# Two experts share one strip of 64 token slots in a mixture-of-experts encoder block

## The chip, the cores and the metric

The kernel runs on one core of a Trainium2 chip. The metric is the device time of one execution in microseconds (us). TensorE multiplies matrices, VectorE (DVE), ScalarE (ACT) and GpSimd (POOL) work elementwise, and SyncE (SP) issues all DMAs of this kernel.

## The reference

One layer of an encoder with 512 tokens of 1024 channels, all in float32. A first half mixes the tokens (a convolution module and a state-space scan, merged by gates). The second half, the one that the change is about, sends every token to two of 64 experts: the best of 8 groups, and in it the best two of 8 experts.

```
def _hier_moe(xt, w_grp, b_grp, w_er, b_er, w1, w3, w2):
    gp = softmax(xt @ w_grp + b_grp);  g_p, g_idx = top_k(gp, 1)
    el = (xt @ w_er + b_er).reshape(t, 8, 8);  el_sel = el of the group chosen
    e_p, e_loc = top_k(softmax(el_sel), 2);  e_p = e_p / sum(e_p)
    weights = g_p * e_p;  e_glob = g_idx * 8 + e_loc
    ...
    def expert_block(args):
        xblk, e = args
        hdn = jax.nn.silu(xblk @ w1[e]) * (xblk @ w3[e])
        return hdn @ w2[e]
    ...
# reference: h = h + g2 * moe;  return rmsnorm(h, final_g)
```

w1[e] and w3[e] are 1024 x 512, w2[e] is 512 x 1024: 6.29 MB an expert, 403 MB for all. With 512 x 2 assignments an expert has 16 tokens on average.

## The kernel before

The first half (some 765 us) computes everything up to h, the residual stream, and hg, the normalized tokens, both with tokens on the partitions. Then the router chooses groups and experts for all tokens on DVE. `pcum` counts, with products of one-hots and a triangular matrix in PSUM, which place a token has in the queue of its expert; the key of an assignment is 512 times its expert plus that place. Every expert has a strip of 64 slots (CAP). Assignments beyond them are counted in `nq`, and a loop behind the main one works them off, with passes of 128 slots that load their expert's weights again; with no such assignment it is skipped.

**The expert loop** (lines 1471 to 1505) goes over 32 pairs of experts. A pair has 128 slots, 64 for each. For each pair:
- `choose` (DVE) makes the one-hot S [tokens, slots] from the keys; `gather` multiplies it with hg on TensorE, 8 steps (k) of 4 products into ps_g, and ACT writes the gathered tokens xg, scaled and shifted, in FP32. From pair 3 on the one-hot is bf16 and hg is split into three bf16 parts by `split`, so that a step has 12 bf16 products in place of 4 FP32 ones.
- `hidden` multiplies 64 columns of xg with w1 and w3 of one expert, 16 products into ps_w; ACT makes the SiLU (`sl`), DVE multiplies. `hidden_t` transposes the result into ps_ht, DVE copies it to `ht`. `second` multiplies ht with w2, 8 products into the two halves ps_y. The second expert of a pair has them crossed, so that each of the two PSUM tiles holds 64 rows of either expert.
- `scale_y` multiplies by the routing weights (tables tabA, tabB by slot) and g2, splits y into two parts yh and yl, and POOL makes `so`, the one-hot back from slots to tokens. `combine` has 8 steps: two products into ps_o and an addition to h on DVE. For the last pair, two of the four token blocks are summed in PSUM instead (ps_f), where `to_psum` puts h.

The generators gather (g, G for the first), combine (c; the `tables` in pair 0), split (x) and to_psum (z) are advanced one step at a time between the matmuls of `hidden`, and while ACT, DVE work on its result. FILL0 to FILL3 and FILL are the lists of these steps: for each expert of the pair, ten places: before each k of `hidden`, after it (place 8) and after `hidden_t` (place 9).

**The weights** come through a ring of 8 buffers of 2 MB (`load_upto`, lines 750 to 775). An expert has 3 blocks: the first and the second half of k of w1 and w3 together, and w2. A load waits until the products that read its buffer last are done. Blocks 8 to 23 and the last expert's are loaded in smaller pieces (`fine`). All loads are issued by SP in order. Six of the first eight blocks are loaded during the first half.

The end (`final`) is the last RMSNorm, per block of 128 tokens, and the store.

Of the kernel before, what the change touches and what calls it, by code (L numbers as in the profile page):

```python
# [129 lines left out]
def hybrid_block(ctx: ExitStack, tc: tile.TileContext, a, out, dbg=None, stage=9):  # L130
# [1130 lines left out]

    def split():
        h1 = tk.tile([P, 4, KD, P], BF, name="hg1", tag="hg1")
        hgb = hg.bitcast(BF).rearrange("p c k (r q) -> p c k r q", r=2)
# [2 lines left out]
        todo = [(c, slice(4 * q, 4 * q + 4)) for q in range(2) for c in range(4)]
        ts = {}
        for n in range(len(todo) + 1):
            if n < len(todo):  # L1270
                i = todo[n]
                S.copy(h1[:, i[0], i[1]], hg[:, i[0], i[1]])
                ts[n] = mo.tile([P, 4, P], F32, name="hs", tag="S", bufs=2)
                V.tensor_sub(ts[n], hg[:, i[0], i[1]], h1[:, i[0], i[1]])
# [430 lines left out]
```

## Time and profile before

| | us |
|---|---|
| median of 3 runs (1839.68 to 1841.95) | 1841.07 |
| the profiled execution | 1842.43 |
| its span, from the first to the last instruction | 1840.6 |
| TensorE busy in it | 1752.0 |
| DVE busy in it | 1067.2 |

The profile is one execution. Its rows give start and duration of instructions, merged where equal ones follow each other, as recorded on each engine; what an engine waited for is inferred from the semaphores. An FP32 matmul of the code has two records. Nearly every TensorE and DVE instruction has line 125, that of a helper, so the tile's name tells which it is.

### The profile page before, as it was taken

To read this page: it belongs to the slowest core of one execution; us is meant where nothing else is said; L and a number is where in the kernel's file an instruction comes from. 1 tells how busy PE (TensorE), PEld (TensorE's weight loads), DVE (VectorE), ACT (ScalarE), POOL (GpSimd) and SP (SyncE) were. 2 spreads that over 40 slices of the span, in tenths; PEclk is the share of its full clock that TensorE was granted. 3 is DMA by queue.
4 is the path that set the end of the run, shared out by engine and by line. 5 is a ranking of instruction groups with operands and counts; after the bars stand their busy time and mean duration, and the time that the engine had idled before them with its cause. 6 is when DMAs were issued, how large, how long until landed. Compare 5 with 4: busy or idle time off the path is not lost.

```text
span 1840.6 us, 25565 instructions
## 1 busy us (share of the span) xinstructions
PE 1752.0 (95%) x10188; PEld 1043.8 (57%) x10188; DVE 1067.2 (58%) x1696; ACT 577.8 (31%) x1045; POOL 398.9 (22%) x272
## 2 busy tenths in 40 slices
PE   5999999989999989899999999999999999999996
PEld 2777778767777777753444444444444444444442
DVE  6889999979998576444343343434343433434344
ACT  2455564636644643522111111111111111111112
POOL 3123331623325354302010101111110101011111
PEclk7999999999999989999999999999999999999998
DMA  6252422515245667478899999999999999999971
GB/s 256 72 163 69 137 92 81 161 60 166 72 144 166 236 206 270 163 301 307 356 389 406 388 409 391 405 392 406 405 391 408 392 404 392 406 391 405 391 318 47
DMA packets 97562, 506.92 MB, mean 275 GB/s; under 512 B 10208, under 2 KB 14560, under 8 KB 51616
## 3 DMA queue, kind: packets, MB, share of 16 engines
q1 hardware_dynamic: 97440, 505.25, 71.5%
q8 instruction: 82, 1.34, 0.3%
q14 instruction: 40, 0.33, 0.1%
HBM read 502.98 MB, written 2.23 MB: 274 GB/s over the span
## 4 chain that ended last, share of the span: by engine, by line
PE 72%; DVE 18%; issue 4%; ACT 2%; DMA 1%; POOL 1%; SPq 0%; DVEq 0%; ACTq 0%; POOLq 0%
PE ps_w L125 24%; PE ps_y L125 13%; PE ps_g L125 10%; PE ps_mm L125 8%; PE ps_o L125 7%; DVE accv L125 6%; DVE w_lo L125 3%; PE ps_ys L125 3%; DVE ct L125 3%; PE ps_cv L125 2%; PE ps_mix L125 2%; DVE xs L125 1%; PE ps_ht L125 1%; PE ps_ada L125 1%; DMA w_raw<-in_w_in_dram 1%
## 5 line engine op out<-in xcount | busy, mean ns | idle before, releaser
L125 PE MATMUL ps_w<-wb,xg 128*64 128x512 f32 x2048 | 470.6, 597 | 0.0
L125 DVE TENSOR_TENSOR h<-h,ps_o 128x512 f32<-128x512 f32 x252 | 168.0, 686 | 286.0 <-PE ps_o L125 286.0
L125 PEld LDWEIGHTS ps_w<-wb,xg 128*64 128x64 f32 x2048 | 138.7, 137 | 268.1 <-issue 265.8
L125 PE MATMUL ps_y<-wb,ht 128*64 128x512 f32 x1024 | 236.5, 604 | 2.5 <-DVE ht L125 2.5
L125 PE MATMUL ps_mm<-n1h,w_lo 128*128 128x512 f32 x560 | 221.9, 396 | 10.0 <-DVE w_lo L125 10.0
L125 PE MATMUL ps_mm<-n1h,w_hi 128*128 128x512 f32 x560 | 227.0, 405 | 0.2 <-ACT w_hi L217 0.2
L125 PE MATMUL ps_mm<-n1l,w_hi 128*128 128x512 f32 x560 | 220.1, 393 | 0.0
L125 DVE SCALAR_TENSOR_TENSOR accv<-u,par,accv 128x494 f32<-128x494 f32 (+29 forms) x240 | 211.1, 916 | 5.4 <-ACT accv L438 2.9
L125 PE MATMUL ps_g<-S,hg 128*128 128x128 bf16 (+1 forms) x2976 | 210.5, 223 | 1.5 <-DVE S L125 1.5
L1307 ACT ACTIVATE sl<-ps_w 128x256 f32<-128x256 f32 x64 | 24.6, 384 | 595.5 <-PE ps_w L125 595.5
L1338 POOL TENSOR_SCALAR so<-par,tabA 128x512 fp32r<-128x512 f32 x32 | 50.0, 1563 | 690.4 <-PE ps_o L125 659.6
L125 PEld LDWEIGHTS <-hg 128*128 128x128 bf16 x2784 | 160.4, 98 | 67.7 <-issue 67.0
L125 DVE TENSOR_TENSOR sl<-sl,ps_w 128x256 f32<-128x256 f32 x64 | 39.1, 610 | 259.1 <-ACT sl L1307 259.1
L217 ACT CAST w_hi<-w_raw 128x1024 fp32r<-128x1024 f32 (+1 forms) x103 | 107.1, 1040 | 250.6 <-PE ps_mm L125 95.0
L125 DVE TENSOR_TENSOR w_lo<-w_raw,w_hi 128x1024 fp32r<-128x1024 f32 (+1 forms) x103 | 135.7, 1318 | 85.2 <-ACT w_hi L217 77.6
L125 PEld LDWEIGHTS ps_y<-wb,ht 128*64 128x64 f32 x1024 | 68.6, 138 | 136.8 <-issue 131.2
L1295 ACT ACTIVATE xg<-ps_g,cB,cG 128x128 f32<-128x128 f32 x256 | 96.4, 456 | 144.7 <-PE ps_g L125 144.7
L125 PEld LDWEIGHTS ps_mm<-n1h,w_lo 128*128 128x128 f32 x560 | 106.3, 190 | 37.1 <-DVE w_lo L125 14.3
L125 PEld LDWEIGHTS ps_mm<-n1h,w_hi 128*128 128x128 f32 x560 | 106.7, 190 | 25.2 <-issue 2.4
L125 PEld LDWEIGHTS ps_mm<-n1l,w_hi 128*128 128x128 f32 x560 | 106.5, 190 | 23.7 <-issue 2.2
L125 PE MATMUL ps_o<-yh,so 128*128 128x512 f32 x252 | 117.1, 465 | 2.0 <-DVE h L125 1.3
L853 POOL TENSOR_TENSOR ada_acc<-ada_acc,ada_w 128x512 f32<-128x512 f32 x56 | 90.0, 1609 | 108.7 <-ACT ada_w L851 106.8
(326 smaller groups left out, 2173.3 us busy)
## 6 DMA issues: line engine op xcount, KB each, us to landing
wb<-in_w_dram SPq DMA_DIRECT2D x244, 1024.0 KB, 8.2
wb<-in_w_dram SPq DMA_DIRECT2D x57, 2048.0 KB, 10.0
w_raw<-in_w_in_dram SPq DMA_DIRECT2D x72, 512.0 KB, 3.6
wb<-in_w_dram SPq DMA_DIRECT2D x52, 512.0 KB, 7.0
ada_w<-in_w_ada_dram SPq DMA_DIRECT2D x64, 256.0 KB, 3.7
ada_w<-in_w_ada_dram SPq DMA_DIRECT2D x16, 512.0 KB, 9.0
mE<-sdram SPq DMA_DIRECT2D x32, 256.0 KB, 6.4
w_raw<-in_w_ssm_dram SPq DMA_DIRECT2D x16, 512.0 KB, 3.5
```

The source lines that it names most:

```text
L125: return f(*args, **kw)
L217: S.copy(hi[:, :n], raw[:, :n])
L853: G.tensor_add(acc, acc, w)
L1295: S.activation(xg[:, q], ps[:, i], AF.Identity, bias=cB2[:, q:q + 1], scale=cG2[:, q:q + 1])
L1307: S.activation(sl, ps[:, 0], AF.Silu)
L1338: G.tensor_scalar(st, tok, tabs2[x][0], None, op0=OP.is_equal)
```

## The change

Experts e and e + 32 share one strip of 64 slots: the tokens of e + 32 take the places behind those of e. A turn of the loop now has four experts (e, e + 32, e + 1, e + 33) with 128 slots, and there are 16 turns. One gather, one scale_y and one combine serve all four. `ORDER` gives the order of the experts for loads and products. Each of two experts in a strip multiplies all its 64 columns; the product behind the SiLU multiplies by a mask by slot (`own`: 1 where the slot is the expert's) as well, and `second` adds both experts of a strip up in the same PSUM rows. The counts `pcum` get a fifth row with the totals, and the totals of the experts e are added to the places of e + 32. The key goes by strips (`hi_` folds the upper four groups onto the lower). The bf16 split of hg is gone; all gathers are FP32 with 4 products a step. The lists of fillers are new. The loop behind takes up to 31 passes, with keys set back to experts (kx) and FP32 gathers.

```diff
@@ -747,15 +747,19 @@
             pool.tile([P, 2, 4, T], F32, name=f"wz{q}", tag=f"b{q}")
         return pool

+
+    ORDER = [e + f for q in range(NE // 4) for e in (2 * q, 2 * q + 1) for f in (0, NE // 2)]
+
     def load_upto(n):
         while len(wblocks) <= min(n, 3 * NE - 1):
             b = len(wblocks)
-            e, part = divmod(b, 3)
+            o, part = divmod(b, 3)
+            e = ORDER[o]
             pool, tag = SEQ[b % NB]
             if b < NB:
                 wring.append(wpools[pool].tile([P, 4 * D], F32, name=f"wb{b}", tag=tag))
             t = wring[b % NB]
-            fine = NB <= b < HB or e == NE - 1
+            fine = NB <= b < HB or o == NE - 1
...
@@ -920,6 +924,8 @@
         io(c_("slot2", [P, 2, CAP]), [[512, 2], [1, CAP]], 0, 0)
         io(c_("slotd", [P, 2, CAP]), [[0, 2], [1, CAP]], 0, 0)
         io(c_("tokp", [P, 4]), [[P, 4]], 1, 1)
+        io(c_("slotp", [P, 1]), [[0, 1]], 1, 1)
+        G.tensor_scalar(B_["slotp"][64:P], B_["slotp"][64:P], -64.0, None, op0=OP.add)
...
@@ -1192,14 +1198,22 @@
     warm_up(WARM2)
     S.activation(eg, eg, AF.Exp)
     S.activation(ee, ee, AF.Exp)
-    pcum = py.tile([P, 4, NE], F32, name="ps_cum", tag="y")
+
+    H = NE // 2
+    pcum = py.tile([P, 5, NE], F32, name="ps_cum", tag="y")
     for c in range(4):
         for b in range(c):
-            PE.matmul(pcum[:, c], lhsT=oneb, rhs=ohv[:, b], start=(b == 0), stop=False)
-        PE.matmul(pcum[:, c], lhsT=tri, rhs=ohv[:, c], start=(c == 0), stop=True)
+            PE.matmul(pcum[:, c], lhsT=oneb, rhs=ohv[:, b], start=False, stop=False)
+        PE.matmul(pcum[:, c], lhsT=tri, rhs=ohv[:, c], start=(c == 0), stop=False)
+    for b in range(4):
+        PE.matmul(pcum[:, 4], lhsT=oneb, rhs=ohv[:, b], start=False, stop=False)
+    for b in range(4):
+        PE.matmul(pcum[:, :, H:], lhsT=oneb, rhs=b8(ohv[:, b, None, :H], [P, 5, H]), start=False, stop=(b == 3))
     tokens_to(8, WT2)

-    kb = r_("kb", [P, 2, 4, 1])
+    kb, hi_ = r_("kb", [P, 2, 4, 1]), tk.tile([P, 4, 1], F32, name="hi_")
+    V.tensor_scalar(hi_, g_mi, 4.0, 4.0, op0=OP.is_le, op1=OP.mult)
+    V.tensor_add(g_mi, g_mi, hi_)
     for j in range(2):
         V.scalar_tensor_tensor(kb[:, j], g_mi, 8.0, mi_[:, j], op0=OP.mult, op1=OP.add)
     V.tensor_scalar(kb, kb, -512.0, 512.0 * 72, op0=OP.mult, op1=OP.add)
@@ -1219,6 +1233,12 @@
         yield

     in_turns(places)
+
+    own, tot = tk.tile([P, 2, H], F32, name="own"), tk.tile([P, NE], F32, name="tot")
+    V.tensor_copy(tot, pcum[:, 4])
+    for f, op in enumerate((OP.is_ge, OP.is_lt)):
+        V.tensor_scalar(own[:, f], tot[:, :H], B_["slotp"], None, op0=op)
+    own = own.rearrange("p f e -> p (f e)")
...
@@ -1253,30 +1273,7 @@
     def choose(p):
         rel = mt_("rel", [P, 2, 4, 1], 2)
         V.tensor_scalar(rel, key, -1024.0 * p, None, op0=OP.add)
-        return onehot(rel, slot2f, dt=BF if p >= FIRST else F32)
-
-
-    FIRST = 3
-    parts = []
-
-    def split():
-        h1 = tk.tile([P, 4, KD, P], BF, name="hg1", tag="hg1")
-        hgb = hg.bitcast(BF).rearrange("p c k (r q) -> p c k r q", r=2)
-        h2, h3 = hgb[:, :, :, 0], hgb[:, :, :, 1]
-        parts[:] = [h1, h2, h3]
...
-            if n:
-                i = todo[n - 1]
-                S.copy(h2[:, i[0], i[1]], ts[n - 1])
-                G.tensor_sub(h3[:, i[0], i[1]], ts[n - 1], h2[:, i[0], i[1]])
-            yield
+        return onehot(rel, slot2f)

...
@@ -1286,16 +1283,14 @@
             if k % 4 == 0:
                 ps = pg.tile([P, 4, P], F32, name="ps_g", tag="g")
             for c in range(4):
-                hs = [t[:, c, k] for t in parts] or [hg[:, c, k]]
-                for r, t in enumerate(hs):
-                    PE.matmul(ps[:, k % 4], lhsT=t, rhs=s[:, c], start=(c == 0 and r == 0), stop=(c == 3 and t is hs[-1]))
+                PE.matmul(ps[:, k % 4], lhsT=hg[:, c, k], rhs=s[:, c], start=(c == 0), stop=(c == 3))
...
@@ -1305,8 +1300,8 @@
         t = mt_("sl", [P, 512], 1)
         sl, hd_ = t[:, :256], t[:, 256:].rearrange("p (r q) -> p r q", r=2)
         S.activation(sl, ps[:, 0], AF.Silu)
-        V.tensor_mul(hd_.rearrange("p r q -> p q r"), sl.rearrange("p (q r) -> p q r", r=2),
-                     ps[:, 1].rearrange("p (q r) -> p q r", r=2))
+        V.scalar_tensor_tensor(hd_.rearrange("p r q -> p q r"), sl.rearrange("p (q r) -> p q r", r=2), mine,
+                               ps[:, 1].rearrange("p (q r) -> p q r", r=2), op0=OP.mult, op1=OP.mult)
         return hd_

     def hidden_t(hd_):
@@ -1317,14 +1312,14 @@
         V.tensor_copy(ht.rearrange("p r j s -> p r (j s)"), pt)
         return ht

-    def second(ht, e, w, yps):
+    def second(ht, e, f, w, yps):
         n = 0
         for j in range(2):
             for r2 in range(2):
                 for x in range(2):
                     half = x ^ e
                     PE.matmul(yps[half][64 * x:64 * x + 64], lhsT=ht[:, r2, j], rhs=w[2][:, j, r2, half * T:(half + 1) * T],
-                              start=(n == 0), stop=(n == 3))
+                              start=(n == 0 and f == 0), stop=(n == 3 and f == 1))
...
-
-
-    FILL0 = [v.split(",") for v in "GG,GG,,c,,,g,,gg,g;cc,gcc,c,gc,c,c,c,,gg,cc".split(";")]
-    FILL1 = [v.split(",") for v in ",,,,g,g,g,g,gg,gg;cx,xc,xc,xc,xc,xc,xc,xc,xc,".split(";")]
-    FILL2 = [v.split(",") for v in "x,x,x,x,c,c,c,,c,;c,g,gc,g,gc,g,gc,g,g,gc".split(";")]
-    FILL3 = [v.split(",") for v in ",c,c,c,c,c,c,c,,;c,,,,,,,,z,z".split(";")]
-    FILL = [v.split(",") for v in ",,,,cgcc,,,,gg,gc;,,cgcc,,,,,,gg,gc".split(";")]
+    nq4 = NE // 4 if stage > 5 else 2
+
+
+    FILL0 = [v.split(",") for v in "GG,GG,,c,,c,,,cc,c;,,c,,c,,,gg,c,c;,,,c,,,,gg,c,c;,,,,,,,,gg,gg".split(";")]
+    FILL3 = [v.split(",") for v in ",,,,,,,,cc,cc;,,,,,,,,cc,cc;,,,,,,,,,;,,,,,,,,z,z".split(";")]
+    FILL = [v.split(",") for v in ",,,,,,,,gg,cc;,,,,,,,,gg,cc;,,,,,,,,gg,cc;,,,,,,,,gg,cc".split(";")]
...
@@ -1441,19 +1434,19 @@
                 yield


-        tab[:] = [tk.tile([P, 2, NE // 2], F32, name="tabA"), tk.tile([P, 2, NE // 2], F32, name="tabB")]
-        pv = ptab.rearrange("p a (q r) -> p a q r", r=2)
+        tab[:] = [tk.tile([P, 2, NE // 4], F32, name="tabA"), tk.tile([P, 2, NE // 4], F32, name="tabB")]
+        ts = r_("ts", [P, 2, H])
+        V.tensor_copy(ts, ptab[:, :, :H])
+        V.tensor_add(ts, ts, ptab[:, :, H:])
+        pv = ts.rearrange("p a (q r) -> p a q r", r=2)
         for x in range(2):
             for r2 in range(2):
                 V.tensor_copy(tab[x][64 * r2:64 * r2 + 64], pv[64 * r2:64 * r2 + 64, :, :, r2 ^ x])
         yield

-        pall = po_.tile([P, NE], F32, name="ps_all", tag="o")
-        for b in range(4):
-            PE.matmul(pall, lhsT=oneb, rhs=ohv[:, b], start=(b == 0), stop=(b == 3))
-        V.tensor_scalar(nq, pall, float(CAP), None, op0=OP.is_gt)
+        V.tensor_scalar(nq, tot, float(CAP), None, op0=OP.is_gt)
         for q in range(1, 4):
-            V.scalar_tensor_tensor(nq, pall, float(CAP + 128 * q), nq, op0=OP.is_gt, op1=OP.add)
+            V.scalar_tensor_tensor(nq, tot, float(CAP + 128 * q), nq, op0=OP.is_gt, op1=OP.add)
...

-    pend, sp_ = None, split()
-    for p in range(npair):
-        yps, fl_ = yps_(), FILL3 if p == npair - 1 else (FILL0, FILL1, FILL2, FILL)[min(p, 3)]
-        more = {"c": combine(pend) if pend else tb, "g": iter(()), "x": sp_, "G": g0, "z": to_psum()}
-        if p + 1 < npair and p != FIRST - 1:
+    pend = None
+    for p in range(nq4):
+        yps, fl_ = yps_(), FILL3 if p == nq4 - 1 else FILL if p else FILL0
+        more = {"c": combine(pend) if pend else tb, "g": iter(()), "G": g0, "z": to_psum()}
+        if p + 1 < nq4:
             more["g"] = gather(sn)
             xn = next(more["g"])

@@ -1479,27 +1472,23 @@
             for n in names:
                 next(more[n], None)

-        for e in range(2):
-            b = 3 * (2 * p + e)
-            load_upto(b + NB - 1)
-            w = wblocks[b:b + 3]
-            hd_ = hidden(xg, e, w, lambda k: fill(fl_[e][k]))
-            if p == npair - 1 and e:
+        for i in range(4):
+            e, f = divmod(i, 2)
+            o = 4 * p + i
+            load_upto(3 * o + NB - 1)
+            w = wblocks[3 * o:3 * o + 3]
+            hd_ = hidden(xg, e, w, own[:, ORDER[o]:ORDER[o] + 1], lambda k: fill(fl_[i][k]))
+            if p == nq4 - 1 and i == 3:
                 S.activation(mt_("dummy", [P, 1], 1), epsc, AF.Sqrt)
-            fill(fl_[e][8])
+            fill(fl_[i][8])
             ht = hidden_t(hd_)
-            fill(fl_[e][9])
-            if p == FIRST - 1 and not e:
-                steps(sp_, 16)
-                sn = choose(FIRST)
-                more["g"] = gather(sn)
-                xn = next(more["g"])
-            second(ht, e, w, yps)
+            fill(fl_[i][9])
+            second(ht, e, f, w, yps)
         for n in "cg":
             steps(more[n], 16)
-        if p == npair - 1:
+        if p == nq4 - 1:
             steps(more["z"], 3)
-        if p != FIRST - 2 and p + 2 < npair:
+        if p + 2 < nq4:
             sn = choose(p + 2)
         pend = scale_y(yps, [(tab[x][:, 0, p:p + 1], tab[x][:, 1, p:p + 1]) for x in range(2)])
...
             V.tensor_copy(oint[:, 0:1], cend[0:1, NE - 1:NE])
+            kx = ow.tile([P, 2, 4, 1], F32, name="kx")
+            for j in range(2):
+                V.scalar_tensor_tensor(kx[:, j], hi_, 128.0 * H, key[:, j], op0=OP.mult, op1=OP.add)
```

## Rows read from the trace of the kernel before

**Rows 1.** The page: the span, the busy time of the engines (share of the span, instructions), and GB/s moved in 40 equal slices of the span.
```profile
span 1840.6 us, 25565 instructions
...
PE 1752.0 (95%) x10188; PEld 1043.8 (57%) x10188; DVE 1067.2 (58%) x1696; ACT 577.8 (31%) x1045; POOL 398.9 (22%) x272
...
GB/s 256 72 163 69 137 92 81 161 60 166 72 144 166 236 206 270 163 301 307 356 389 406 388 409 391 405 392 406 405 391 408 392 404 392 406 391 405 391 318 47
```

**Rows 2.** Busy time of each engine by stretch: start:end and length in us, busy us (instructions) of PE, PEld, DVE, ACT and POOL, granted TensorE clock as a share of full speed, DMA share, GB/s. The stretches are the first experts, the rest of the loop, its end, and the final part.
```profile
792.50:905.00 112.50, 107.41 (x576) 46.46 (x572) 45.08 (x109) 23.83 (x52) 19.42 (x14) 0.97 0.86 324
905.00:1780.00 875.00, 875.00 (x5866) 407.80 (x5864) 344.33 (x684) 137.38 (x329) 85.94 (x55) 1.00 0.99 399
1780.00:1820.00 40.00, 37.39 (x179) 13.28 (x178) 12.18 (x20) 5.38 (x11) 4.69 (x3) 1.00 0.13 42
1820.00:1841.00 21.00, 6.26 (x20) 3.07 (x18) 13.33 (x31) 10.88 (x20) 5.01 (x4) 0.75 0.27 102
```

**Rows 3.** Waits of the DMA queue of SP from 850 to 1790 us: line of the load, what it waited for, us in total, times, the longest.
```profile
SPq L763 <- PE ps_y L125: 295.0, 116, 4.5
SPq L763 <- PE ps_w L125: 248.0, 61, 7.2
```

**Rows 4.** TensorE in order of time, some 13 us of one pair: start us, duration us, line, operation, tiles, array rows x columns, shape, records.
```profile
1204.88 0.48 PE L125 MATMUL ps_o<-yh,so 128*128 128x512 f32 x1
...
1205.43 0.39 PE L125 MATMUL ps_o<-yh,so 128*128 128x512 f32 x1
...
1205.99 5.37 PE L125 MATMUL ps_w<-wb,xg 128*64 128x512 f32 x24
1211.30 1.51 PE L125 MATMUL ps_g<-S,hg 128*128 128x128 bf16 x24
1212.65 0.39 PE L125 MATMUL ps_ht<-ident,sl 128*128 128x128 f32 x2
...
1213.51 0.48 PE L125 MATMUL ps_o<-yh,so 128*128 128x512 f32 x1
...
1214.16 3.65 PE L125 MATMUL ps_y<-wb,ht 128*64 128x512 f32 x16
```

**Rows 5.** The DMA queue of SP in order of time: start us and us of the loads of w1 and w3 of three experts that follow each other.
```profile
1211.40 6.78 SPq L763 DMA_DIRECT2D wb<-in_w_dram  x4
...
1227.20 6.78 SPq L763 DMA_DIRECT2D wb<-in_w_dram  x4
...
1243.00 6.78 SPq L763 DMA_DIRECT2D wb<-in_w_dram  x4
```

**Rows 6.** TensorE in order of time: the first gather, in FP32, and the first product of the loop.
```profile
780.98 5.74 PE L125 MATMUL ps_g<-S,hg 128*128 128x128 f32 x48 [1.47 <-DVE S L125]
786.65 1.08 PE L125 MATMUL ps_w<-wb,xg 128*64 128x512 f32 x4
```

**Rows 7.** Stretches as in rows 2: the first and the last of 25 stretches of 24.5 us that lie 31.6 us apart (the period of a pair), a stretch of 2 us between two of them, and one behind the last load of weights.
```profile
960.70:985.20 24.50, 24.50 (x156) 11.10 (x155) 10.98 (x23) 4.63 (x11) 1.73 (x2) 1.00 1.01 420
...
1719.10:1743.60 24.50, 24.50 (x156) 11.10 (x155) 10.98 (x23) 4.63 (x11) 1.73 (x2) 1.00 1.01 422
...
1208.00:1210.00 2.00, 2.00 (x12) 0.67 (x10) 0.00 (x0) 0.00 (x0) 0.00 (x0) 1.00 0.79 176
...
1788.00:1790.00 2.00, 1.62 (x6) 0.57 (x6) 1.95 (x4) 0.69 (x2) 0.00 (x0) 1.00 0.04 8
```

**Rows 8.** The DMA queue of SP in order of time: the load of block 8, the first that waits for an expert's products, and the last load of weights.
```profile
792.48 0.80 SPq L772 DMA_DIRECT2D wb<-in_w_dram  x2
...
1772.56 5.49 SPq L769 DMA_DIRECT2D wb<-in_w_dram  x4
```

**Rows 9.** The end of the loop in order of time: the last products into ps_y, the next instruction of TensorE, and the scaling on DVE that they release (in brackets its idle time before and what ended it).
```profile
1816.11 3.65 PE L125 MATMUL ps_y<-wb,ht 128*64 128x512 f32 x16
...
1819.69 1.98 PE L125 MATMUL ps_f<-h,ident 128*128 128x512 f32 x4
1819.81 0.75 DVE L125 SCALAR_TENSOR_TENSOR y<-ps_y,tabA,g2row 128x512 f32<-128x512 f32 x1 [4.03 <-PE ps_y L125]
```

**Rows 10.** The pair after split: two instructions of TensorE with the idle time before them, and two stretches as in rows 2.
```profile
857.84 0.69 PE L125 MATMUL ps_ht<-ident,sl 128*128 128x128 f32 x2 [2.19 <-DVE sl L125]
859.04 6.29 PE L125 MATMUL ps_y<-wb,ht 128*64 128x512 f32 x16 [0.52 <-DVE ht L125]
...
857.00:860.00 3.00, 1.64 (x6) 0.63 (x8) 1.21 (x3) 0.33 (x1) 3.00 (x3) 0.59 1.02 367
860.00:863.00 3.00, 3.00 (x10) 0.90 (x8) 0.00 (x0) 0.00 (x0) 1.88 (x2) 0.50 0.57 183
```

**Rows 11.** Groups of instructions from 780 us on: line, engine, operation, tiles, shapes, count, busy us, mean ns of one, idle us before them and what ended it. The SiLU and the product behind it.
```profile
L125 DVE TENSOR_TENSOR sl<-sl,ps_w 128x256 f32<-128x256 f32 x64 | 39.1, 610 | 259.1 <-ACT sl L1307 259.1
...
L1307 ACT ACTIVATE sl<-ps_w 128x256 f32<-128x256 f32 x64 | 24.6, 384 | 595.5 <-PE ps_w L125 595.5
```

**Rows 12.** TensorE in the last pair, first expert, which has no filler behind `hidden` and `hidden_t`: idle time before an instruction in brackets.
```profile
1801.46 0.44 PE L125 MATMUL ps_ht<-ident,sl 128*128 128x128 f32 x2 [1.12 <-DVE sl L125]
1802.42 3.65 PE L125 MATMUL ps_y<-wb,ht 128*64 128x512 f32 x16 [0.52 <-DVE ht L125]
```

**Rows 13.** Groups on DVE between 760 and 790 us, the router: the instruction that reads the counts pcum.
```profile
L125 DVE TENSOR_TENSOR rt<-ps_cum,rt 128x128 f32<-128x128 f32 x2 | 0.5, 281 | 0.0
```

More of the change, by code (lines that the diff above doesn't have):

```diff
@@ L766, in load_upto @@
                 w2 = a["w2"][e].rearrange("(j p r) d -> p j r d", j=2, r=2)
-                if e == NE - 1:
+                if o == NE - 1:
                     for j, r in [(0, 0), (0, 1), (1, 0), (1, 1)]:
@@ L1242, in hybrid_block, with onehot @@
     tok_iota = lambda t: G.iota(t, pattern=[[1, T]], base=1, channel_multiplier=0, allow_small_or_imprecise_dtypes=True)
-    def onehot(rel, iota, tag="S", dt=F32):
-        s = mo.tile([P, 4, P], dt, name="S", tag=tag, bufs=2)
+    def onehot(rel, iota, tag="S"):
+        s = mo.tile([P, 4, P], F32, name="S", tag=tag, bufs=2)
         for c in range(4):
@@ L1255, in choose @@
         V.tensor_scalar(rel, key, -1024.0 * p, None, op0=OP.add)
-        return onehot(rel, slot2f, dt=BF if p >= FIRST else F32)
-    FIRST = 3
-    parts = []
-    def split():
-        h1 = tk.tile([P, 4, KD, P], BF, name="hg1", tag="hg1")
-        hgb = hg.bitcast(BF).rearrange("p c k (r q) -> p c k r q", r=2)
-        h2, h3 = hgb[:, :, :, 0], hgb[:, :, :, 1]
-        parts[:] = [h1, h2, h3]
[L1267 to L1274, printed above, removed]
-            if n:
-                i = todo[n - 1]
-                S.copy(h2[:, i[0], i[1]], ts[n - 1])
-                G.tensor_sub(h3[:, i[0], i[1]], ts[n - 1], h2[:, i[0], i[1]])
-            yield
+        return onehot(rel, slot2f)
     def gather(s):
@@ L1296, in gather, with hidden @@
             yield
-    def hidden(xg, e, w, fill):
+    def hidden(xg, e, w, mine, fill):
         ps = pw.tile([P, 2, 256], F32, name="ps_w", tag="w")
@@ L1555, in hybrid_block @@
     man.close()
-    n_extra = nc.values_load(cnt_[0:1, 0:1], min_val=0, max_val=15)
+    n_extra = nc.values_load(cnt_[0:1, 0:1], min_val=0, max_val=31)
     with tc.If(n_extra > 0):
@@ L1570, in hybrid_block @@
+            G.iota(i32, pattern=[[1, 32]], base=0, channel_multiplier=0, allow_small_or_imprecise_dtypes=True)
+            le = ow.tile([P, 32, NE], F32, name="le")
+            V.tensor_tensor(le, b8(cend[:, None, :], [P, 32, NE]), b8(i32[:, :, None], [P, 32, NE]), op=OP.is_le)
+            oe = ow.tile([P, 32, 1], F32, name="oe")
             V.reduce_sum(oe, le, axis=AX.X)
-            V.tensor_tensor(le, le, b8(nq[:, None, :], [P, 16, NE]), op=OP.mult)
-            cs = ow.tile([P, 16, 1], F32, name="cs")
+            V.tensor_tensor(le, le, b8(nq[:, None, :], [P, 32, NE]), op=OP.mult)
@@ L1573, in hybrid_block @@
+            cs = ow.tile([P, 32, 1], F32, name="cs")
             V.reduce_sum(cs, le, axis=AX.X)
-            obase = ow.tile([P, 17], F32, name="obase")
+            obase = ow.tile([P, 33], F32, name="obase")
             V.memset(obase, 0.0)
-            t16 = ow.tile([P, 16], F32, name="t16")
-            V.tensor_tensor(t16, i16, cs[:, :, 0], op=OP.subtract)
-            V.tensor_scalar(t16, t16, 128.0, float(CAP), op0=OP.mult, op1=OP.add)
-            V.scalar_tensor_tensor(obase[:, 0:16], oe[:, :, 0], 512.0, t16, op0=OP.mult, op1=OP.add)
@@ L1580, in hybrid_block @@
-            oint = ow.tile([1, 17], I32, name="oint")
-            V.tensor_scalar(oint[:, 1:17], oe[0:1, :, 0], float(NE - 1), None, op0=OP.min)
+            t32 = ow.tile([P, 32], F32, name="t32")
+            V.tensor_tensor(t32, i32, cs[:, :, 0], op=OP.subtract)
+            V.tensor_scalar(t32, t32, 128.0, float(CAP), op0=OP.mult, op1=OP.add)
+            V.scalar_tensor_tensor(obase[:, 0:32], oe[:, :, 0], 512.0, t32, op0=OP.mult, op1=OP.add)
+            oint = ow.tile([1, 33], I32, name="oint")
@@ L1590, in hybrid_block @@
                 rel = o_("orel", [P, 2, 4, 1])
-                V.tensor_scalar(rel, key, obase[:, 0:1], None, op0=OP.subtract)
+                V.tensor_scalar(rel, kx, obase[:, 0:1], None, op0=OP.subtract)
                 sj = o_("osj", [P, 4, 2, P])
-                s2_ = o_("os2", [P, 4, P], BF)
+                s2_ = o_("os2", [P, 4, P])
                 iot = o_("oiot", [P, P])
@@ L1613, in hybrid_block @@
                     for c in range(4):
-                        for r in range(3):
-                            PE.matmul(ps, lhsT=parts[r][:, c, k], rhs=s2_[:, c], start=(c + r == 0), stop=(c + r == 5))
+                        PE.matmul(ps, lhsT=hg[:, c, k], rhs=s2_[:, c], start=(c == 0), stop=(c == 3))
                     S.activation(xg[:, k], ps, AF.Identity, bias=cB2[:, k:k + 1], scale=cG2[:, k:k + 1])
@@ L1639, in hybrid_block @@
                         V.tensor_add(hv, hv, ps)
-                nb = o_("onb", [P, 16])
-                V.tensor_copy(nb, obase[:, 1:17])
-                V.tensor_copy(obase[:, 0:16], nb)
+                nb = o_("onb", [P, 32])
+                V.tensor_copy(nb, obase[:, 1:33])
+                V.tensor_copy(obase[:, 0:32], nb)
         with tc.tile_pool(name="fn", bufs=1, side="right") as fn:
```

8 lines of the change are left out of this document (2 added, 6 removed).

## The prediction

> **What bounds the kernel now.** I read the page first, then the stretches by stage, then the waits of the DMA queue, then one pair of experts in order of time, and last the two ends of the weight stream. The page shows TensorE busy 95% of the span and the bytes per second close to 400 GB/s from the middle on [rows 1]. By stage, the expert loop from 905 to 1780 us is the place: TensorE is busy 875.00 of 875 us and the DMA engines have a share of 0.99 at 399 GB/s [rows 2]. Two engines look full, so the question is which waits for which. The DMA queue's own waits answer it: the loads wait for TensorE to finish with a ring buffer, 295.0 us after products into ps_y and 248.0 us after products into ps_w in these two groups alone [rows 3]; TensorE has no idle time there at all. So TensorE bounds the loop and the stream follows it. The loads of successive experts start at 1211.40, 1227.20 and 1243.00 us [rows 5]: 15.80 us per expert, 31.60 us per pair.
>
> The stream stands close behind. One expert is 3 blocks of 2.097 MB, 6.291 MB. In stretches of 24.5 us in which the queue is not empty, the first and the last of 25 that lie 31.6 us apart, the DMA moves 420 and 422 GB/s at a share of 1.01; the missing bytes are in short holes such as 1208 to 1210 us, with 176 GB/s [rows 7], where the next load still waits for its buffer. At 421 GB/s an expert takes 14.94 us. That is the floor behind the present bound, only 0.86 us (5%) under it.
>
> **What a page says to this.** The row shows 399 GB/s over 875 us and 421 in the full stretches [rows 2, 7]. The Trainium skill, "DMA: Bandwidth & Descriptors", section "Bandwidth", says of loads from HBM that a limit of about 358 GB/s per core binds. By it the 385.9 MB below would need 1078 us and no TensorE saving could help. The trace moves more than that already, so the measurement decides, the rule gets no chance of its own, and the sum goes by the rows.
>
> **The change, part by part: TensorE in the loop.** An FP32 matmul has two records in the trace (ps_w: 1024 in the code, 2048 records). Removed per pair: 96 bf16 gather products; 24 of them take 1.35 us (1211.30 to 1212.65) [rows 4], so 5.3 us, 2.65 us per expert. Added per four experts: 32 FP32 gather products. The trace has them in the first gather: 48 records, 24 products, from 780.98 to 786.65 us [rows 6], 0.236 us each, so 7.6 us, 1.89 us per expert. The combination's two products per step take 0.55 us (1204.88 to 1205.43) to 0.65 us (1213.51 to 1214.16) [rows 4]; 8 steps are about 4.7 us, 2.35 us per expert before and 1.17 us after. ps_w, ps_y and the transposes stay. TensorE then needs 15.80 - 2.65 + 1.89 - 1.17 = 13.9 us per expert, 1.0 us under the 14.94 us of the stream. The bound passes from TensorE to the DMA, and what TensorE saves beyond 0.86 us per expert is not seen.
>
> The mask in the product behind the SiLU turns a TENSOR_TENSOR of 610 ns [rows 11] into a SCALAR_TENSOR_TENSOR over the same elements; I count it between 0 and +0.15 us. With ACT's 0.38 us before it this chain is about 1.2 us, and TensorE has two gather steps (8 products, 1.9 us) to do in the meantime in each of the four experts; the copy of ht behind it is covered by two combination steps (1.2 us). Without cover the two gaps are 1.12 and 0.52 us [rows 12]. Halving scale_y, choose, the h additions and the so tiles frees DVE, ACT and POOL, which bound nothing there: 0. The order of the experts only changes load addresses: 0.
>
> **Before the loop.** DVE is the path between the running counts and the first one-hot. It gains two small instructions on g_mi, and the copy of tot and two comparisons: five at up to 0.28 us, the nearest row [rows 13]. With eight short bf16 products hidden in between I take +1.4 us (0 to 2), which shifts the start of the loop.
>
> **The first experts.** split() goes, and with it the stretch around 855 to 866 us in which TensorE waited 2.19 and 0.52 us and then ran at a granted clock of 0.50 [rows 10]. From 792.5 to 905 us the stream averages 324 GB/s [rows 2], because TensorE frees buffers late. Against 421 this loses 112.5 x (1 - 324/421) = 26 us. I walked through the first four experts with the new fillers: about 15, 15, 15 and 15 us, 60 in place of 78 (786.65 to 865.2), and every buffer comes free 1 to 2 us before the stream wants it. A thin queue still has short holes. I take 4 us of loss in all; the bounds are 0 and the 26 us of now.
>
> **The sum.** The first load that waits for an expert's products starts at 792.48 us [rows 8]; with the shift, 793.9. It is block 8 of 192, so 184 blocks, 385.9 MB, follow: 917 us at 421 GB/s. With 4 us of holes, and 2 us for the last piece to be signalled, the last weight lands at 1717 us. Before, the last weight is issued by 1778.05 us [rows 8] and the DMA is empty at 1788 [rows 7], but the last product of ps_y ends only at 1819.7 [rows 9]: TensorE is up to 8 blocks behind. After, it waits for the last quarter of w2 and needs about 1 us more. From that product to the end of the span are 1840.6 - 1819.7 = 20.9 us [rows 1, 9], in which scaling, combination and the final norm stay as they are. 1717 + 1 + 20.9 = 1739 us of span, 101.6 us less. The profiled execution took 1842.43 us beside its span of 1840.6, so 1740.8 us; it lies 1.4 us over the median of the runs, which leaves 1739.5. I say 1740 us.
>
> Where the saving sits: 26 - 4 us in the first experts, about 0.86 us in each of some 55 later ones (47 us), and some 32 us of TensorE's lag behind the last load, which there is none of any more.
>
> **The rivals.**
> 1. *A fuller queue doesn't hold 421 GB/s.* If the holes were the DMA's own rests and 399 GB/s its sustained rate, 385.9 MB take 967 us: 1790 us. For it: the share is 0.99 already. Against it: every one of the 25 stretches has 419 to 422, and each hole follows a wait for TensorE. Chance 0.08.
> 2. *The gaps are not covered.* If the fillers come too late, 1.12 + 0.52 us [rows 12] per expert bring TensorE to 15.5 us, and it stays the bound: 64 x 0.3 = 19 us in the loop and some 20 us at its start, about 1800 us. From 2 us of gaps per expert on there is no gain in the loop. Against it: the fillers are 1.9 and 1.2 us. Chance 0.04, 0.02 of it for no change at all.
> 3. *The clock, and the time ends above today's.* TensorE now waits for data, about 1 us per expert. Rows show a fall: after gaps of 2.19 and 0.52 us the granted clock is 0.59 and 0.50, the 1.2 GHz level, and sixteen records of ps_y take 6.29 us in place of 3.65 [rows 4, 10]. If it fell in every expert's wait and stayed down, TensorE would be the bound again; slower than today from a mean granted clock of 13.9/15.8 = 0.88 on. At 0.75 an expert takes 18.5 us and the loop is 64 x 2.7 = 173 us longer, about 2010 us. Against it: gaps of 1.12 and 0.52 us beside each other left the clock whole between 1780 and 1820 us [rows 2, 12], and a TensorE that slows stops waiting, with eight blocks of ring before the stream feels it. Chance 0.02. [...]
> 4. *The strip overflows.* A pair of experts with over 64 slots needs an extra pass behind the loop with its own 6.3 MB and a second final norm, at least 15 + 21 us. By the reference's routing of its drawn inputs the fullest pair has 57. Chance 0.01, and one pass alone would still end under today's time.
>
> **How the numbers follow.** Forecast: 0.85. Its own range comes from the unknown terms: 0 to 26 us of holes, 0 to 2 of shift, 1% of rate (9 us): 1730 to 1770. With rival 1 outside it the range still holds 8 in 10; I give 1730 to 1772. A change of 0.2% (3.7 us) is about what the runs can tell. Faster by more: 0.85 + 0.08 + 0.02 + 0.01 = 0.96; the same: 0.02; slower: 0.02.
>
> **What would show it.** After the change the waits of the DMA queue for TensorE should be gone from the middle of the loop, TensorE should wait for loads of wb, about 1 us per expert at a granted clock near 1.00, the stretches of the loop should read 419 to 422 GB/s throughout, and an expert should take 14.9 us. The first loop stretch up to 905 us should read about 400 GB/s. ps_g should have 1024 records, all FP32; ps_o and so half of theirs; the last product of ps_y should end about 1 us behind the last load. Wrong it would be with 400 GB/s in the loop and an always busy TensorE, or with a granted clock under 0.9 there.

## The result and the profile after

The changed kernel takes 1760.38 us (4 runs, 1759.38 to 1761.28), the kernel before 1840.89 us (4 runs, 1839.68 to 1841.95): a ratio of 0.9563, 95% interval 0.9546 to 0.9579, 80.5 us less. The prediction was 1740 us, 1730 to 1772.

The page after: the span, busy times, GB/s by slice, the costliest product with its idle time, and the most frequent load of weights with its count, size and median us from issue to landing; last, the row of the same loads from the page of the kernel before.

```profile
span 1759.5 us, 20528 instructions
...
PE 1614.3 (92%) x7984; PEld 964.4 (55%) x7984; DVE 896.3 (51%) x1359; ACT 500.9 (28%) x869; POOL 339.9 (19%) x234
...
GB/s 268 63 171 72 94 134 72 167 73 72 167 84 180 160 234 220 302 133 282 390 419 421 421 421 421 420 421 421 421 421 420 421 421 421 421 420 421 421 421 184
...
L125 PE MATMUL ps_w<-wb,xg 128*64 128x512 f32 x2048 | 462.0, 594 | 51.2 <-DMA wb<-in_w_dram 51.2
...
wb<-in_w_dram SPq DMA_DIRECT2D x244, 1024.0 KB, 22.3
...
wb<-in_w_dram SPq DMA_DIRECT2D x244, 1024.0 KB, 8.2
```

Against [rows 1] the loop reads 419 to 421 GB/s in every slice from the 21st to the 39th, where it had swung between 388 and 409. TensorE now waits, 51.2 us in all, and for loads; before, it waited for none in the loop. A 1 MB load lands 22.3 us after its issue; in the kernel before this was 8.2 us. The queue is full where it used to run dry.

Busy time by stretch, with the columns of [rows 2]: turn 0 (from the first load that waits for an expert), the next three experts, the loop, its end, and the final part.

```profile
799.00:861.00 62.00, 53.99 (x262) 22.78 (x260) 12.02 (x50) 4.43 (x12) 3.13 (x2) 0.94 0.95 351
861.00:905.00 44.00, 44.00 (x228) 19.19 (x226) 9.89 (x16) 3.89 (x9) 0.00 (x0) 1.00 1.02 417
...
905.00:1080.00 175.00, 175.00 (x906) 78.00 (x904) 51.08 (x102) 19.27 (x48) 12.62 (x8) 1.00 1.01 420
1080.00:1700.00 620.00, 571.30 (x2883) 252.88 (x2881) 153.07 (x290) 59.37 (x143) 31.51 (x20) 1.00 1.01 421
...
1700.00:1737.00 37.00, 32.40 (x137) 10.70 (x134) 5.68 (x11) 2.63 (x5) 3.10 (x2) 1.00 0.83 337
1737.00:1760.00 23.00, 6.24 (x20) 3.08 (x18) 13.29 (x31) 10.87 (x20) 4.99 (x4) 0.70 0.25 94
```

There are three phases. In turn 0 the stream is short of free buffers (351 GB/s). Up to 1080 us TensorE is still busy all the time while the stream runs at its full rate: TensorE is faster and eats up the lead that the eight loaded buffers gave. From 1080 us on it waits for data, and the rate doesn't change by it.

TensorE in order of time: the products into ps_w of three experts that follow each other, before and after that point (the number in brackets is idle time just before).

```profile
861.61 7.04 PE L125 MATMUL ps_w<-wb,xg 128*64 128x512 f32 x32
...
875.19 7.04 PE L125 MATMUL ps_w<-wb,xg 128*64 128x512 f32 x32
...
888.78 7.04 PE L125 MATMUL ps_w<-wb,xg 128*64 128x512 f32 x32
...
1697.37 3.65 PE L125 MATMUL ps_w<-wb,xg 128*64 128x512 f32 x16 [1.36 <-DMA wb<-in_w_dram]
...
1712.28 3.65 PE L125 MATMUL ps_w<-wb,xg 128*64 128x512 f32 x16 [1.21 <-DMA wb<-in_w_dram]
```

An expert takes TensorE 13.59 us (861.61 to 875.19 to 888.78) when it has its data, and 14.91 us (1697.37 to 1712.28) when it must wait: the 14.94 us of the stream, in place of 15.80 [rows 5].

### The profile page after: what moved, and what is told of

Its sections match the earlier page's. It is cut to its first block, busy times and chain, and to the rows that moved or that the text cites. A ratio compares the mean times of both kernels' runs of the same rounds, so it can differ in the third digit from the quotient of the medians.

```text
span 1759.5 us, 20528 instructions
## 1 busy us (share of the span) xinstructions
PE 1614.3 (92%) x7984; PEld 964.4 (55%) x7984; DVE 896.3 (51%) x1359; ACT 500.9 (28%) x869; POOL 339.9 (19%) x234
## 4 chain that ended last, share of the span: by engine, by line
DMA 39%; PE 37%; DVE 16%; issue 4%; ACT 2%; POOL 2%; SPq 0%; DVEq 0%; ACTq 0%; POOLq 0%
DMA wb<-in_w_dram 37%; PE ps_mm L125 10%; PE ps_w L125 8%; PE ps_y L125 5%; DVE accv L125 5%; DVE w_lo L125 3%; PE ps_ys L125 3%; PE ps_g L125 3%; PE ps_cv L125 3%; PE ps_mix L125 2%; DVE ct L125 2%; PE ps_o L125 1%; DVE mE L125 1%; PE ps_ada L125 1%; DVE xs L125 1%
## 5 line engine op out<-in xcount | busy, mean ns | idle before, releaser
L125 PE MATMUL ps_w<-wb,xg 128*64 128x512 f32 x2048 | 462.0, 594 | 51.2 <-DMA wb<-in_w_dram 51.2
L125 DVE SCALAR_TENSOR_TENSOR sl<-sl,own,ps_w 128x256 f32<-128x256 f32 x64 | 42.8, 669 | 632.4 <-ACT sl L1302 632.4
L125 PEld LDWEIGHTS ps_w<-wb,xg 128*64 128x64 f32 x2048 | 151.5, 137 | 346.1 <-issue 329.6
L125 DVE SCALAR_TENSOR_TENSOR accv<-u,par,accv 128x494 f32<-128x494 f32 (+29 forms) x240 | 207.3, 900 | 5.4 <-ACT accv L438 2.9
L1333 POOL TENSOR_SCALAR so<-par,tabA 128x512 fp32r<-128x512 f32 x16 | 25.0, 1563 | 870.6 <-PE ps_o L125 828.7
L125 PEld LDWEIGHTS ps_g<-S,hg 128*128 128x128 f32 x1024 | 121.7, 195 | 51.9 <-issue 48.7
L125 PE MATMUL ps_g<-S,hg 128*128 128x128 f32 x1024 | 133.7, 285 | 2.7 <-DVE S L125 2.7
L125 PE MATMUL ps_ys<-yhl,w_hi 128*128 128x512 f32 x256 | 85.7, 417 | 8.5 <-DVE accy L125 8.4
L125 DVE TENSOR_TENSOR h<-h,ps_o 128x512 f32<-128x512 f32 x124 | 79.6, 683 | 2.6
L1290 ACT ACTIVATE xg<-ps_g,cB,cG 128x128 f32<-128x128 f32 x128 | 48.1, 456 | 72.8 <-PE ps_g L125 72.8
## 6 DMA issues: line engine op xcount, KB each, us to landing
wb<-in_w_dram SPq DMA_DIRECT2D x244, 1024.0 KB, 22.3
```

The costliest lines, as they stand in the source:

```text
L125: return f(*args, **kw)
L1290: S.activation(xg[:, q], ps[:, i], AF.Identity, bias=cB2[:, q:q + 1], scale=cG2[:, q:q + 1])
L1333: G.tensor_scalar(st, tok, tabs2[x][0], None, op0=OP.is_equal)
```

## The experiments

Two theories. **A:** the weight stream bounds the loop, at 421 GB/s; TensorE has 1.35 us to spare per expert, and only what delays the stream itself, at its start, reaches the end. **B:** TensorE still sets the time, with stalls and clock in place of the work removed. Then a second question: why 1760 and not 1740.

### More work for TensorE: e1_plus1, e2_plus3, e9_plus3_turns

```diff
         for k in range(KD):
             fill(k)
             for j in range(2):
+                for r in range(again if k == 0 else 0):
+                    PE.matmul(ps[64 * j:64 * j + 64], ..., start=True, stop=True)
                 PE.matmul(ps[64 * j:64 * j + 64], ..., start=(k == 0), stop=(k == KD - 1))
...
-            hd_ = hidden(..., lambda k: fill(fl_[i][k]))
+            hd_ = hidden(..., lambda k: fill(fl_[i][k]), again=1 if p else 0)
```

Expected of one copy: 

> The changed kernel, with the first two products of ps_w of every expert done twice from turn 1 on (the first copy is overwritten): 0.86 us of TensorE more for each of 60 experts. Theory A, the weight stream bounds the loop and TensorE has 14.94 - 13.59 = 1.35 us to spare per expert: the time stays within 2 us of 1760. Theory B, TensorE still sets the time (its stalls and clock made up for what was removed): 60 x 0.86 = 52 us more, about 1812 us.

Measured: 1760.29 us (2 runs, 1756.61 to 1763.96). The rows show the added work and that it cost nothing. First two experts of this kernel in order of time, then its loop as in [rows 2]:

```profile
1300.31 7.94 PE L125 MATMUL ps_w<-wb,xg 128*64 128x512 f32 x36
...
1314.80 7.95 PE L125 MATMUL ps_w<-wb,xg 128*64 128x512 f32 x36
...
905.00:1700.00 795.00, 792.21 (x4019) 385.43 (x4020) 205.76 (x394) 78.75 (x190) 44.18 (x28) 1.00 1.01 421
```

14.49 us per expert, 0.90 more than before the copy and still under 14.94; TensorE is busy 792 of 795 us, and its waits for loads fall to 3.4 us from 905 us on. The stream keeps 421 GB/s. So 54 us of TensorE time went in for free: theory B falls. It is also a warning for reading a page: by its TensorE share alone this kernel looks bound by TensorE, and its time is that of the stream.

Expected of three copies (again=3): 

> The same with three copies, 2.58 us more per expert. Theory A: TensorE then needs 13.59 + 2.58 = 16.17 us per expert, over the 14.94 of the stream, and bounds the loop again: from 861.6 us 60 x 16.17 less some 7 for the last turn without a gather, then 23 us of end, so about 1848 us (1840 to 1856). Theory B: 60 x 2.58 = 155 us more, about 1915 us.

Measured: 1958.55 us, over both. The rows show a dearer copy.

```profile
1309.05 11.38 PE L125 MATMUL ps_w<-wb,xg 128*64 128x512 f32 x44
...
1326.97 6.29 PE L125 MATMUL ps_w<-wb,xg 128*64 128x512 f32 x24
...
905.00:1900.00 995.00, 994.73 (x4536) 435.15 (x4533) 209.95 (x401) 79.44 (x192) 47.23 (x30) 1.00 0.88 351
```

An expert takes 17.92 us, 4.33 more, and not the 2.58 that I had put in. My copies came three in a row for one half of the array, with the kernel's own product four, before the other half's; the products of the kernel alternate between the two halves. Whether this was the price needed a run of its own, with the two loops exchanged so that the copies alternate:

```diff
-            for j in range(2):
-                for r in range(again if k == 0 else 0):
+            for r in range(again if k == 0 else 0):
+                for j in range(2):
                     PE.matmul(ps[64 * j:64 * j + 64], ..., start=True, stop=True)
```

> As e2_plus3, with the copies for the two halves of the array in turns, so that they overlap as the products of the kernel do and cost 0.86 us each: 2.58 us per expert in place of the 4.33 that e2_plus3 shows. Theory A: TensorE bounds the loop at 16.17 us per expert; e3_half_w2 gives the time of the loop when TensorE alone bounds it, 1699 us, and 60 x 2.58 = 155 us more make 1854 us (1848 to 1862), with no waits for loads in the loop. If the price of a copy isn't what made e2_plus3 dearer, but something that comes with a loop bound by TensorE, it stays near 1958 us.

Measured: 1852.93 us (1852.24 to 1852.93).

```profile
1314.71 9.61 PE L125 MATMUL ps_w<-wb,xg 128*64 128x512 f32 x44
1330.86 5.32 PE L125 MATMUL ps_w<-wb,xg 128*64 128x512 f32 x24
...
905.00:1700.00 795.00, 795.00 (x4042) 340.47 (x4043) 185.30 (x357) 71.31 (x173) 39.24 (x25) 1.00 0.98 390
```

An expert takes 16.15 us, TensorE never waits and the stream follows it at 390 GB/s, as it followed at 399 before the change. With the next run's 1699 us for a loop bound by TensorE alone, 60 x 2.58 and 60 x 4.33 us give 1854 and 1959 us for the two; measured were 1853 and 1959. The copies show in the time only above the stream's 14.94 us: at 14.49 us per expert (one copy) not at all, at 16.15 us in full, as theory A has it.

### Fewer bytes: e3_half_w2

```diff
                 else:
-                    SP.dma_start(t, w2)
+                    SP.dma_start(t if b < NB else t[:, 0], w2 if b < NB else w2[:, 0])
```

> The changed kernel, which leaves out the loads of the second half of w2 for 55 experts (the products read what an earlier load left there): 57.7 MB less, all other work as it is. Theory A: the stream alone would end 137 us earlier, so TensorE bounds the loop at 13.59 us per expert: 861.6 + 60 x 13.59 - 7 + 23, about 1694 us (1688 to 1702), without waits for loads. Theory B: the bytes don't matter, 1760 us.

Measured: 1699.22 us. The loop as in [rows 2], and two experts in order of time:

```profile
905.00:1640.00 735.00, 734.86 (x3778) 325.68 (x3776) 203.98 (x391) 78.59 (x190) 44.12 (x28) 1.00 1.00 389
...
1309.58 7.04 PE L125 MATMUL ps_w<-wb,xg 128*64 128x512 f32 x32
...
1323.16 7.04 PE L125 MATMUL ps_w<-wb,xg 128*64 128x512 f32 x32
```

With fewer bytes and the same instructions the time falls by 61 us and an expert takes 13.58 us: the loop is bound by TensorE again. So the bytes were the bound after the change, and 1699 us is what the change's TensorE saving would have been worth without them.

### One half of the saving alone: e4_no_combine

The kernel before, with the combination of 27 pairs left out:

```diff
-        more = {"c": combine(pend) if pend else tb, ...}
+        more = {"c": (iter(()) if 3 < p < npair - 1 else combine(pend)) if pend else tb, ...}
```

> The kernel before the change, with the combination of pairs 3 to 29 left out (27 of 32): the gathers stay as they were. TensorE needs 15.80 - 2.35 = 13.45 us per expert. Theory A: the stream bounds: 36 MB are moved by 905 us as in the kernel before, the other 349 MB take 830 us, and with 2 us for the last piece, 2 to the last product and 22 to the end this gives about 1761 us (1755 to 1768), the same as the change, though the other half of its saving is not there. Theory B, TensorE sets the time: 27 x 4.7 = 127 us less than before, about 1714 us.

Measured: 1777.53 us in the profiled run and 1787.09 in the other, above both, and nearer to A. The loop as in [rows 2]:

```profile
905.00:1720.00 815.00, 779.87 (x5473) 351.94 (x5471) 195.40 (x471) 139.25 (x334) 87.87 (x56) 1.00 1.01 419
```

419 GB/s with waits of TensorE for loads, as after the change. The 15 us over A's 1761 come from what I had not counted: from 905 to 1100 us the stream still read 415 GB/s, and the last pair keeps its eight combination steps between the products, so its first expert takes 19.5 us (1720.3 to 1739.9) and the last product ends at 1752.9 in place of some 1739. Of TensorE's saving of 127 us, 54 to 64 show in the time; A had asked for 80, B for all. With two runs 10 us apart the amount is uncertain; the rate and the waits speak for A.

### When a delay counts: e5_late_turn0, e6_late_turn8

The copies of e2_plus3 in one turn alone: `again=3 if p == 0 else 0`, and `again=3 if p == 8 else 0`.

> The changed kernel with 2.58 us of TensorE more for each of the four experts of turn 0 alone, 10.3 us in all. Theory A (what is lost in turn 0 leaves holes in the weight stream that nothing gives back): about 10 us more, 1768 to 1772. Rival (the thin stream of the first turn is the DMA's own start, not TensorE's lateness): 0 to 3 us more.

> The same 10.3 us, put into turn 8. Theory A: the ring has seven loads queued there, and the stream runs on: 0 to 1 us more, 1760 to 1761. Rival (every microsecond of TensorE counts): 10 us more.

Measured: 1771.74 us (4 runs, 1770.97 to 1777.32) and 1760.51 us (1756.83 to 1761.02). As above a turn cost 4 x 4.33 = 17.3 us and not 10.3. In turn 0 (790.82 to 875.02 us, 15.8 us longer than in the changed kernel) this made the time 11.4 us longer (12.1 us in the two profiles from the first product of the loop to the end of the span), and the stream read 292 to 300 GB/s from 799 to 860 us; in turn 8 it cost nothing, though there it was the same work. The first product of turn 0 and of turn 1 with the copies in turn 0; then two experts of turn 8, and the stretch of that turn, with the copies there:

```profile
790.82 5.42 PE L125 MATMUL ps_w<-wb,xg 128*64 128x512 f32 x16
...
875.02 7.04 PE L125 MATMUL ps_w<-wb,xg 128*64 128x512 f32 x32
...
1312.33 11.38 PE L125 MATMUL ps_w<-wb,xg 128*64 128x512 f32 x44
1330.25 7.04 PE L125 MATMUL ps_w<-wb,xg 128*64 128x512 f32 x32
...
1280.00:1360.00 80.00, 80.00 (x389) 35.31 (x388) 17.42 (x33) 7.66 (x19) 3.16 (x2) 1.00 1.01 421
```

TensorE is fully busy for these 80 us and the stream reads 421 GB/s: the ring had loads enough in the queue. In these two places lateness counted where the queue was thin, and not where it was full.

### The missing microseconds of turn 0: e7_fill, e8_fill_warm

```diff
-    FILL0 = [... "GG,GG,,c,,c,,,cc,c;,,c,,c,,,gg,c,c;,,,c,,,,gg,c,c;,,,,,,,,gg,gg" ...]
+    FILL0 = [... "GG,GG,,c,,c,,c,g,g;,c,,c,,c,,c,g,g;,c,,c,,,,,g,g;,c,,c,,,,,g,g" ...]
```

> The changed kernel with other fillers in turn 0: the steps of the tables, for which TensorE waited behind hidden and hidden_t, go between the products, and a gather step goes into each of these places. Theory A: turn 0 takes about 59 us in place of 68.4, and the time falls by 6 to 9 us, to 1751 to 1754. Rival (the holes are the DMA's own): 0 to 2 us less.

Measured: 1752.61 us (4 runs, 1751.42 to 1754.63), 7.8 us less than the changed kernel, at 0.9511 of the time before (0.9490 to 0.9531). Its turn 0 in the profile, the first product and the first of turn 1, and the same 62 us as in the first row of the stretches above:

```profile
790.75 1.08 PE L125 MATMUL ps_w<-wb,xg 128*64 128x512 f32 x4
...
849.35 7.04 PE L125 MATMUL ps_w<-wb,xg 128*64 128x512 f32 x32
...
796.50:858.50 62.00, 61.62 (x317) 26.61 (x314) 15.67 (x52) 6.17 (x15) 3.13 (x2) 1.00 0.98 392
```

Turn 0 takes 58.6 us in place of 68.4, and the stream reads 392 GB/s there in place of 351, which is 62 x 41 / 421 = 6 us of stream. The holes were TensorE's lateness, not the DMA's own start. Not all of the 7.8 us need be the fillers': in this profile the loop also starts 2.4 us earlier than in the changed kernel's (790.75 against 793.18). From the first product of the loop to the end of the span it takes 960.0 us (1750.7 - 790.75), against 966.3 in the changed kernel and 965.2 in e6_late_turn8 (1758.4 - 793.21), whose first gather is as fast as here. So 5 to 6 us are turn 0's, as the rate says.

e8 adds `WARM3 = 8` and moves the two mask instructions behind `sn = choose(1)`.

> As e7_fill, with eight small products on TensorE while it waits for the first one-hot, and the mask made behind the first two one-hots in place of ahead of them. Theory A: the first gather runs at the full clock (46 records in 5.4 us in place of 7.8) and starts 0.4 us earlier; every us of it comes off the end: 2 to 3 us less than e7_fill. Rival: the clock's loss is hidden, no difference to e7_fill.

Measured: 1751.20 us (1749.81 to 1754.37), which can't be told from e7_fill. The premise failed: the first gather of e7_fill already ran its 48 records in 5.74 us, at the full clock, and the one of e8 in 5.52. It is slow in the profiles of the changed kernel, of e1_plus1 and of e3_half_w2 (7.8 to 8.0 us for 46 records), and at the full clock in the five others with the same instructions up to there. So this run says nothing on whether such a loss comes off the end.

## Why the prediction came out as it did

The mechanism was right for the loop. Predicted for TensorE were 13.9 us per expert, measured 13.59 (a slip of 0.05 us is in the sum: four times 1.35 us are 5.4 us per pair, not 5.3). The stream was to hold 421 GB/s with a full queue; it does, in a row of 620 us. The bound passed to the DMA, the saving is capped at the distance between two bounds, and TensorE's lag behind the last load is gone. Rival 1 (399 GB/s) fell with that row. The limit of about 358 GB/s per core in the Trainium skill, "DMA: Bandwidth & Descriptors", section "Bandwidth", doesn't bind here; the row has 421. The same section gives that limit for each of two cores that share a memory domain and both stream, and 425 GB/s for a core alone; this kernel runs on one core, so the prediction had taken the limit without its condition. Rival 3, the clock: TensorE waits 48 times from 1080 us on, and the granted clock is 1.00 throughout; waits of up to 1.4 us in an expert don't bring it down here, so the throttling by waits for DMA that the Trainium skill tells of ("TensorE: Matmul & The Clock Gate", section "HAM oscillation — how this bites in real kernels") is not seen in the loop. The waits for DMA in the kernel of that section are longer, some 3 to 5 us. Rival 2 was right for turn 0 and wrong for the rest.

The span came out 20.5 us over the 1739 predicted. That the time still lies in the range is in part luck: the range was made of holes, shift and rate, and the last two terms below, 9.3 us, are in none of these. Term by term:

**The start, 5.1 us.** The first load that waits for an expert starts at 799.01, not at 793.9. The loads of the first half already run 2.0 us later in this execution (the last load of x starts at 747.91; in the trace before at 745.90), with the same instructions; in the profiles of the experiments on the changed kernel it starts 0.4 us earlier (e3_half_w2) to 3.7 us later (e1_plus1) than here, so this term varies between executions. The router takes 1.1 us more (predicted 1.4). The rest is the first gather:

```profile
799.01 0.81 SPq L776 DMA_DIRECT2D wb<-in_w_dram  x2
...
784.12 0.79 PE L125 MATMUL ps_g<-S,hg 128*128 128x128 f32 x2 [2.20 <-DVE S L125]
785.43 7.82 PE L125 MATMUL ps_g<-S,hg 128*128 128x128 f32 x46 [0.52 <-DVE S L125]
793.18 1.08 PE L125 MATMUL ps_w<-wb,xg 128*64 128x512 f32 x4
```

9.1 us from its first product to the loop where [rows 6] has 5.7. The granted clock is 0.83 between 780 and 800 us, after idle times of 2.20 and 0.52 us. In five of the experiments (e2, e5, e6, e7, e9) the same gather ran in 5.74 or 5.75 us, after one wait of some 1.5 us. In these five the clock fell some us ahead of the gather (to 0.50 between 782 and 784 us in e6_late_turn8); the kernel before has 1.00 from 770 to 794 us. What in the change brings the fall is not shown.

**Turn 0, 6.3 us.** The step that failed is the walk through the first four experts: I took 60 us, the trace has 68.4 (793.18 to 861.61), and so the holes are 62 x (1 - 351/421) = 10.3 us and not 4. The rows of TensorE and of DVE in the first expert show what I passed over; the last two rows, from the last turn, have the same wait with no filler in it:

```profile
804.58 1.01 PE L125 MATMUL ps_tok<-sv 128*128 128x128 f32 x4 [1.61 <-DVE sv L125]
805.43 0.38 PE L125 MATMUL ps_ht<-ident,sl 128*128 128x128 f32 x2
806.85 0.49 PE L125 MATMUL ps_tok<-sv 128*128 128x128 f32 x2 [1.04 <-DVE sv L125]
807.27 5.35 PE L125 MATMUL ps_y<-wb,ht 128*64 128x512 f32 x16
...
803.43 0.66 DVE L125 SCALAR_TENSOR_TENSOR sl<-sl,own,ps_w 128x256 f32<-128x256 f32 x1 [10.85 <-ACT sl L1302]
803.93 0.27 DVE L125 TENSOR_SCALAR sv<-slotd,rt 128x128 f32<-128x128 f32 x1
804.12 0.25 DVE L125 TENSOR_SCALAR sv<-OH,tokp 128x64 f32<-128x64 f32 x1
804.28 0.25 DVE L125 TENSOR_SCALAR sv<-OH,wts 128x64 f32<-128x64 f32 x1
...
1716.39 0.66 DVE L125 SCALAR_TENSOR_TENSOR sl<-sl,own,ps_w 128x256 f32<-128x256 f32 x1 [11.60 <-ACT sl L1302]
...
1717.10 0.44 PE L125 MATMUL ps_ht<-ident,sl 128*128 128x128 f32 x2 [1.17 <-DVE sl L125]
```

A filler that should give TensorE work while DVE is busy was itself a step of `tables`, which needs three DVE instructions first, and these stand in DVE's order behind the masked product that TensorE waits for. So the filler was itself late and stood in front of the transposes: in the last turn they start 0.71 us after the masked product does (1716.39 to 1717.10), here 2.00 us (803.43 to 805.43). The next filler held up the products into ps_y in the same way. Four such waits make 5.3 us, the count `nq` in the third expert 1.6 and the copy of ht behind it 1.1 more, and after them the ps_y rows take 5.35 and 5.04 us in place of 3.65, with a granted clock of 0.72 from 807 to 813 us and of 0.79 from 840 to 848 us. I had counted a filler as cover without asking which engine it needs first. e7_fill, with gather steps in those places, has turn 0 in 58.6 us and is 7.8 us faster, 5 to 6 of them from turn 0.

**The end of the stream, 7.4 us.** From 799.0, 917 us of bytes and 10.7 us of holes (10.3 in turn 0 and 0.4 up to 905 us) lead to 1726; the last product into ps_y ends at 1736.7. I had 3 us for that.

```profile
1728.74 1.94 PE L125 MATMUL ps_w<-wb,xg 128*64 128x512 f32 x8 [0.52 <-DMA wb<-in_w_dram]
...
1733.09 3.65 PE L125 MATMUL ps_y<-wb,ht 128*64 128x512 f32 x16
1736.67 1.98 PE L125 MATMUL ps_f<-h,ident 128*128 128x512 f32 x4
...
1726.00:1728.00 2.00, 1.72 (x8) 0.57 (x8) 0.00 (x0) 0.00 (x0) 0.00 (x0) 1.00 0.88 358
1728.00:1730.00 2.00, 1.48 (x8) 0.48 (x8) 0.00 (x0) 0.00 (x0) 0.00 (x0) 1.00 0.74 301
1730.00:1732.00 2.00, 1.87 (x7) 0.44 (x4) 0.66 (x1) 1.25 (x2) 0.00 (x0) 1.00 0.53 217
```

The rate falls as the queue empties (358, 301, then 217 GB/s), and the last expert's chain begins with the last piece of w1 and w3, not with the last quarter of w2: its products, SiLU, mask, transposes, copy and all of ps_y take 7.9 us (1728.74 to 1736.67), and no product into ps_y waits for w2. This term is read from the rows; no run tests it.

**Behind the last product, 1.9 us.** From 1736.67 to the end of the span are 22.8 us, before 20.9. Up to DVE's last instruction both have 16.2 us. Behind it SP waits for TensorE's sequencer (PEq), at the skipped loop behind the main one (what waits, for what; us, times, the longest):

```profile
SPq L1692 <- PEq L1548: 1.8, 1, 1.8
```

The profile before doesn't have this wait; nor do e2, e5, e6 and e9, where the end takes 21.2 to 21.4 us. With it, in e1, e3, e7, e8 and also in e4, an experiment on the kernel before, it takes 22.4 to 22.8 us. So most of the 1.9 us comes with this wait and not with the change; what the sequencer does in it stays open.

5.1 + 6.3 + 7.4 + 1.9 = 20.7 us, against 20.5. With turn 0 one sign failed too: the stream up to 905 us was to read about 400 GB/s, and it read 379 from 799 us on.

## What to carry to other kernels

When an engine bounds a loop, look for the next bound in the rows before pricing a saving: here it stood 5% behind, and of 2.2 us saved per expert 0.86 counted; half of the saving would have moved the loop to the same bound. In a loop bound by a prefetched stream, time lost while the ring is being drained for the first time is mostly lost for good (15.8 us in turn 0 cost 11.4), and the same work put into one later turn was free here, so spend care on the first turn and on the last. A filler covers a wait only if its own inputs don't stand behind that wait on the engine that is waited for.
